# A two-layer diffusion transformer on one core: the build-time clock steps engines when they come free, and loads of gated values keep to three pairs ahead of weights

## The chip, the cores and the metric

The kernel runs on one core of one Trainium2 chip. The core has TensorE (PE, matmuls), VectorE (DVE), ScalarE (ACT), GpSimd (POOL) and SyncE (SP, which here issues DMAs). The metric is the device time of one execution in microseconds; the median of three runs counts.

## The reference

Two transformer layers over 1024 latent tokens and 256 context tokens of width 1024, in fp32. Layer 0 attends in a neighbourhood, layer 1 with grouped queries. Each is followed by a SwiGLU feed-forward of 2816 hidden features; the context runs through the one of layer 0 alone.

```python
def swiglu_ffn(h, w_in, w_out):
    a, g = jnp.split(h @ w_in, 2, axis=-1)
    return (jax.nn.silu(a) * g) @ w_out
...
    for i in range(DEPTH):
        ...
        a_l = ada_norm(h, norm_mix[i], sh1_l, sc1_l)
        ...
        h = h + g1_l * y_l
        h = h + g2_l * swiglu_ffn(ada_norm(h, norm_ffn[i], sh2_l, sc2_l), ffn_w_in[i], ffn_w_out[i])
        if ctx_out:
            hc = hc + g1_c * y_c
            hc = hc + g2_c * swiglu_ffn(ada_norm(hc, norm_ffn[i], sh2_c, sc2_c), ffn_w_in[i], ffn_w_out[i])
    return rms_norm(h, norm_final)
```

## The kernel before

**Stages.** The span goes through the start and layer 0's attention (to about 767 us), layer 0's feed-forward, called FFN0 here (767 to 1697), layer 1's attention (to 2370) and FFN1 (to the end). The change touches the two feed-forwards and the norms at their borders.

**Arithmetic.** A tile x is split into a high part (a cast on ACT to fp32r: `ah` for activations, `wh` for weights, in lines L1189 and L1431) and a low part x − high (`al`, `wl`: L949 on POOL or L952 on DVE, both in the helper `combine`). A product of two fp32 tiles is three fp32r matmuls: high·high, low·high, high·low (L1455 to L1457 in the first stage of a feed-forward, L1698 to L1700 in the second, L1476 to L1478 and L1351 to L1353 for the context).

**A feed-forward.** Both stages split their matrices in 2x2 blocks and form seven products instead of eight from sums and differences of blocks (`PARTS`). The first stage (`mm1`) goes over 22 hidden blocks and writes gated values through `store` to DRAM, as `FA` and `FT` of eleven pairs of hidden blocks. The second (`mm2`) goes over the seven products in the order P7, P1, P6, P3, P2, P5, P4 (`ORDER2`) and, in each, over the eleven pairs; a pair of a product is 12 matmuls of 128x512. For each pair `load_t` loads a gated value and `load_w` one or two weight tiles (`in_fout`); `weight2` and `value2` make high and low parts of them. P7 takes two weight tiles a pair, P1 one.

**Norms.** `norm` squares the columns (L157), adds squares on DVE or POOL (L144), sums over partitions with a matmul by ones (L190, in `ms_sum`), takes Ln and Exp on ACT (L177, L179) and applies the result (L1170, L1180 in a feed-forward; `apply_norm` with L211 and L131 to L134 for layer 1). b=0 and b=1 are the two halves of 512 latent tokens, ctx the context. Silu of the context's hidden blocks is L1322.

**What sets the order.** Each engine runs its instructions in the order in which the program was written, and the program is written by a planner at build time, `Lanes` (here `bg`). It has a clock `bg.now` in ns, a time at which each engine is taken to come free (`busy`), and a list of small generators (a split, a sum, a load), each of which waits for an engine's letter: T and M for matmuls, L and A for ACT, D for DVE, G for POOL. "GD" is given to whichever of POOL and DVE asks first. `turn` is called once for each matmul product of the feed-forwards and moves the clock by 227 ns; an engine whose `busy` is in the past then writes its next instruction. `both` models that DVE and POOL slow each other when they work side by side. Nothing of the clock exists on the chip; there only the written order counts, with semaphores between engines. DMAs stand in SP's queue, in program order and behind the waits of each.

Of the kernel before, what the change touches and what calls it, by code (L numbers as in the profile page):

```python
# [72 lines left out]
def _build(tc, nc, I, O, top):  # L73
# [110 lines left out]
    def ms_sum(acc, added, count, n, bank, stop=False):  # L184
        while len(added) < count or max(added) > bg.now:
            yield ""
        ms, free = yield from bank()
        yield "M"
        for i in range(2):
            t.matmul(ms[:, :n], lhsT=ones[:], rhs=acc[i], start=i == 0, stop=stop and i == 1)  # L190
        return ms[:, :n], free

    def apply_norm(tag, src, rs, G, sh, ah, al, tmp):
# [3 lines left out]
        def split(kc, x, give):  # L197
            yield "A"
            s.activation(ah[:, kc, :], x, AF.Identity, bias=sh(kc))
            yield "GD"  # L200
            norm_lo(bg.engine == "G", al[:, kc, :], x, sh(kc), ah[:, kc, :].bitcast(F32))
            left.discard(kc)
            if bg.engine == "G":
                bg.cost = 3.7 * x.shape[1]
            yield from bg.sleep(2000 if bg.engine == "G" else 700)
            give()

        for kc in range(KC):
            x, give = yield from tmp.take("nx", rs.shape[1])
            yield "D0"  # L210
            v.scalar_tensor_tensor(x, src(kc), G(kc), rs, ALU.mult, ALU.mult)  # L211
            bg.enter(tag, split(kc, x, give), 800, 1)
# [329 lines left out]
    class Lanes:  # L542
# [60 lines left out]
        def both(self, ns):  # L603

            e, o = ("G", "D") if self.engine == "G" else ("D", "G")
            slow = dict(D=2.17, G=1.19)
            left = max(0.0, self.port[o] - self.now)
# [5 lines left out]
            self.port[e] = self.now + self.cost  # L613
# [21 lines left out]
        def turn(self):  # L635
# [4 lines left out]
            for e in "TMLADG":  # L640
                if self.busy.get(e, 0) <= self.now:
                    self.step(e)
# [374 lines left out]
    class Ffn:  # L1017
# [268 lines left out]
        def ctx_norm(self, tiles, rings):  # L1286
# [5 lines left out]
            at = bg.now + 4000  # L1292
# [76 lines left out]
        def load1(self):  # L1369

            fin = I[f"fin{self.layer}"]
            self.tasks = {}
            for i, (j, names, _) in enumerate(self.todo):
# [241 lines left out]
        def load_t(self):  # L1615

            yield from self.said("feed1")
            for x in ORDER2:
                if x == "P4" and self.layer == 0:
                    self.traw.leave(self.acells1, lambda: self.when.update({"act 1": bg.now}))  # L1620
                for i in range(NP):
                    yield from self.known(("F", i, PARTS[x][1]))
# [5 lines left out]
        def load_w(self):  # L1628

            yield from self.said("load1")  # L1630
            fout = I[f"fout{self.layer}"]
            for x in ORDER2:
                for i in range(NP):
                    for k, half in self.RAW2[x]:
# [3 lines left out]
                        self.when["W", x, i, k, half] = bg.now + 3000  # L1638
            self.when["load w"] = bg.now
# [662 lines left out]
    def load_h():  # L2302
        for kc in range(KC):
            dma(out=ffn0.h[0][kc], in_=H0d[0][:, kc, :])
            ffn0.at[0, kc] = bg.now + 6000
            yield from bg.sleep(1000)
# [320 lines left out]
```

## Time and profile before

| | us |
|---|---|
| median of three runs | 3082.59 (3079.08 to 3083.17) |
| profiled execution, own time | 3080.29 |
| its span | 3078.5 |
| PE busy | 2936.6 (95%) |
| DVE busy | 2339.7 (76%) |
| POOL busy | 1807.9 (59%) |
| ACT busy | 1618.8 (53%) |

The own time is that of the whole execution, the span that from its first to its last instruction. Shares are of the span and are averages over stages with different limits: where PE is busy throughout, work on the other engines is hidden; the time over PE's work is in short stretches in which PE stands still, and these are read one by one from the timeline of PE.

### The profile page before, as it was taken

To read this page: it belongs to the slowest core of one execution; us is meant where nothing else is said; L and a number is where in the kernel's file an instruction comes from. 1 tells how busy PE (TensorE), PEld (TensorE's weight loads), DVE (VectorE), ACT (ScalarE), POOL (GpSimd) and SP (SyncE) were. 2 spreads that over 40 slices of the span, in tenths; PEclk is the share of its full clock that TensorE was granted. 3 is DMA by queue.
4 is the path that set the end of the run, shared out by engine and by line. 5 is a ranking of instruction groups with operands and counts; after the bars stand their busy time and mean duration, and the time that the engine had idled before them with its cause. 6 is when DMAs were issued, how large, how long until landed. Compare 5 with 4: busy or idle time off the path is not lost.

```text
span 3078.5 us, 50271 instructions
## 1 busy us (share of the span) xinstructions
PE 2936.6 (95%) x16460; PEld 2511.9 (82%) x16460; DVE 2339.7 (76%) x4291; ACT 1618.8 (53%) x3736; POOL 1807.9 (59%) x1485
## 2 busy tenths in 40 slices
PE   7999999899999999998998899999999989999998
PEld 4888997788788888887878788888888778888786
DVE  7588778775888776567878588899897787666796
ACT  4345555775642222234455488898886622333444
POOL 4246556775685454356776256666644686555775
PEclk8999999999999999999999999999999999999999
DMA  7777777886434554258655523333323333224963
GB/s 262 218 232 236 226 220 225 241 230 210 171 122 159 192 179 168 74 185 298 201 177 188 171 81 96 98 104 105 106 76 121 130 127 127 103 103 152 321 198 113
DMA packets 307173, 519.05 MB, mean 169 GB/s; under 512 B 46433, under 2 KB 112097, under 8 KB 305121
## 3 DMA queue, kind: packets, MB, share of 16 engines
q1 hardware_dynamic: 306912, 515.84, 51.8%
q8 instruction: 131, 2.15, 0.3%
q14 instruction: 130, 1.06, 0.1%
HBM read 389.61 MB, written 120.18 MB: 166 GB/s over the span
## 4 chain that ended last, share of the span: by engine, by line
PE 75%; DVE 10%; DMA 5%; ACT 3%; POOL 3%; issue 2%; SPq 1%; DVEq 0%; POOLq 0%; ACTq 0%
PE pf L1457 9%; PE pf L1455 9%; PE pf L1456 9%; PE T L864 5%; PE o L495 5%; PE pf L1699 4%; PE pf L1700 4%; PE pf L1698 4%; PE ps L767 3%; PE ps L768 3%; PE ps L769 3%; PE S L2235 2%; DMA K<-Kd 2%; PE S L2236 2%; DVE c L952 1%
## 5 line engine op out<-in xcount | busy, mean ns | idle before, releaser
L857 POOL TENSOR_SCALAR Pt<-Pt,rc 128x1280 f32<-128x1280 f32 (+3 forms) x288 | 299.1, 1039 | 389.8 <-ACT pT L872 139.4
L872 ACT CAST pT<-T 128x256 fp32r<-128x256 f32 (+2 forms) x672 | 304.7, 477 | 125.4 <-PE T L864 121.2
L877 DVE TENSOR_TENSOR pT<-T,pT 128x256 fp32r<-128x256 f32 (+2 forms) x672 | 341.7, 534 | 32.9 <-ACT pT L872 32.4
L864 PE MATMUL T<-ident,Pt 128*128 128x128 f32 x1952 | 304.1, 275 | 22.8 <-POOL Pt L857 22.2
L864 PEld LDWEIGHTS T<-ident,Pt 128*128 128x128 f32 x1952 | 236.6, 141 | 78.7 <-POOL Pt L857 34.0
L495 PE MATMUL o<-pT,Vt 128*128 128x256 f32 x1952 | 296.1, 290 | 2.3 <-DVE pT L877 2.2
L767 PE MATMUL ps<-ah,wh 128*128 128x512 f32 (+1 forms) x688 | 261.2, 380 | 5.4 <-ACT ah L430 2.5
L495 PEld LDWEIGHTS o<-pT,Vt 128*128 128x128 f32 x1952 | 254.8, 189 | 9.3 <-DVE pT L877 5.5
L768 PE MATMUL ps<-al,wh 128*128 128x512 f32 (+1 forms) x688 | 251.7, 366 | 3.9 <-POOL al L132 2.2
L769 PE MATMUL ps<-ah,wl 128*128 128x512 f32 (+1 forms) x688 | 251.0, 365 | 2.8 <-DVE wl L336 2.8
L846 ACT ACTIVATE Pt<-S,rc 128x512 f32<-128x512 f32 (+2 forms) x384 | 247.1, 654 | 9.1 <-DVE rc L838 5.8
L949 POOL TENSOR_TENSOR c<-c,c 128x512 fp32r<-128x512 f32 (+1 forms) x120 | 176.0, 1474 | 91.7 <-ACT c L1431 60.0
L2227 DVE TENSOR_REDUCE nm<-S 128x1 f32<-128x512 f32 x256 | 169.6, 682 | 36.4 <-PE S L2236 34.7
L892 POOL TENSOR_TENSOR r<-ob 128x256 f32<-128x256 f32 x144 | 123.8, 859 | 63.1 <-ACT ob L886 57.3
L952 DVE TENSOR_TENSOR c<-c,c 128x512 fp32r<-128x512 f32 (+1 forms) x111 | 128.2, 1168 | 42.3 <-ACT c L1431 24.7
L846 ACT ACTIVATE Pt<-X,rc 128x256 f32<-128x256 f32 x256 | 125.1, 489 | 65.2 <-DVE rc L838 58.5
L949 POOL TENSOR_TENSOR wl<-c,wh 128x512 fp32r<-128x512 f32 x59 | 81.6, 1385 | 120.3 <-ACT wh L1431 113.5
L1431 ACT CAST wh<-c 128x512 fp32r<-128x512 f32 x111 | 68.6, 619 | 157.4 <-POOL c L949 63.9
L769 PEld LDWEIGHTS ps<-ah,wl 128*128 128x128 f32 x688 | 131.2, 191 | 24.4 <-DVE wl L336 3.3
L767 PEld LDWEIGHTS ps<-ah,wh 128*128 128x128 f32 x688 | 131.6, 191 | 18.7 <-ACT ah L430 2.7
L768 PEld LDWEIGHTS ps<-al,wh 128*128 128x128 f32 x688 | 131.7, 191 | 17.3 <-POOL al L132 4.2
L1455 PE MATMUL pf<-c,wh 128*128 128x512 f32 x372 | 144.9, 390 | 0.0
(613 smaller groups left out, 9734.9 us busy)
## 6 DMA issues: line engine op xcount, KB each, us to landing
c<-in_fout SPq DMA_DIRECT2D x119, 256.0 KB, 3.5
wr<-in_wqkv SPq DMA_DIRECT2D x53, 512.0 KB, 4.3
wr<-in_adaT SPq DMA_DIRECT2D x96, 256.0 KB, 3.1
c<-in_fin SPq DMA_DIRECT2D x68, 256.0 KB, 2.9
adaw<-in_adaT SPq DMA_DIRECT2D x64, 256.0 KB, 3.9
wr<-in_wo SPq DMA_DIRECT2D x32, 512.0 KB, 4.2
wr<-in_fin SPq DMA_DIRECT2D x58, 256.0 KB, 2.9
K<-Kd SPq DMA_DIRECT2D x64, 224.0 KB, 4.5
```

The costliest lines, as they stand in the source:

```text
L495: t.matmul(o_ap, lhsT=u.V[:, kb, :], rhs=u.pT[:, i, :], start=i == 0, stop=i == len(u.blocks) - 1)
L767: t.matmul(ps, lhsT=hi[:, c], rhs=ah[:, kc, :n], start=kc == 0, stop=False)
L768: t.matmul(ps, lhsT=hi[:, c], rhs=al[:, kc, :n], start=False, stop=False)
L769: t.matmul(ps, lhsT=lo[:, c], rhs=ah[:, kc, :n], start=False, stop=kc == KC - 1)
L846: s.activation(u.Pt[:, off:off + u.wid[c]], u.S[c], AF.Exp, bias=u.min, scale=u.sign, accum_out=u.rc[:, 3 + c:4 + c])
L857: g.tensor_scalar(Pt, Pt, u.rc[:, 2:3], 1.0, ALU.mult, ALU.mult)
L864: t.transpose(T[:, i * P:(i + 1) * P], u.Pt[:, (i0 + i) * P:(i0 + i + 1) * P], ident[:])
L872: s.copy(u.pT[:, i0:i0 + n, :P], u.T[c])
L877: v.tensor_tensor(u.pT[:, i0:i0 + n, P:], u.T[c], u.pT[:, i0:i0 + n, :P].bitcast(F32), ALU.subtract)
L1455: t.matmul(ps[:], lhsT=r32(hi[:, c]), rhs=bh, start=k == 0, stop=False)
L1456: t.matmul(ps[:], lhsT=r32(hi[:, c]), rhs=bl, start=False, stop=False)
L1457: t.matmul(ps[:], lhsT=r32(lo[:, c]), rhs=bh, start=False, stop=k == 3)
```

## The change

It has four parts.

- `turn` steps an engine if its `busy` lies at most 226 ns ahead of the clock, not only when it lies behind.
- `both` takes other factors for DVE and POOL side by side (2.25 and 1.3), and starts at the time when the engine comes free. `apply_norm` now counts its operations in it, and `ms_sum` writes the sum's matmuls 1200 ns later than the last add.
- `load_t` loads the value of a pair only once the weights of the pair three before it have been asked for (`seen`).
- Three times of the start are moved: the context's norm (+6000 and the word "h2" said), `load1` of layer 0 (waits for "h2"), and `load_h`.

```diff
--- before.py
+++ after.py
@@ -182,7 +182,7 @@
         give()
 
     def ms_sum(acc, added, count, n, bank, stop=False):
-        while len(added) < count or max(added) > bg.now:
+        while len(added) < count or max(added) + 1200 > bg.now:
             yield ""
         ms, free = yield from bank()
         yield "M"
@@ -200,8 +200,9 @@
             yield "GD"
             norm_lo(bg.engine == "G", al[:, kc, :], x, sh(kc), ah[:, kc, :].bitcast(F32))
             left.discard(kc)
+            bg.both((1290 if bg.engine == "G" else 690) * x.shape[1] / 512)
             if bg.engine == "G":
-                bg.cost = 3.7 * x.shape[1]
+                bg.cost += 1.37 * x.shape[1]
             yield from bg.sleep(2000 if bg.engine == "G" else 700)
             give()
 
@@ -209,6 +210,7 @@
             x, give = yield from tmp.take("nx", rs.shape[1])
             yield "D0"
             v.scalar_tensor_tensor(x, src(kc), G(kc), rs, ALU.mult, ALU.mult)
+            bg.both(690 * x.shape[1] / 512)
             bg.enter(tag, split(kc, x, give), 800, 1)
         while left:
             yield ""
@@ -603,14 +605,15 @@
         def both(self, ns):
 
             e, o = ("G", "D") if self.engine == "G" else ("D", "G")
-            slow = dict(D=2.17, G=1.19)
-            left = max(0.0, self.port[o] - self.now)
+            slow = dict(D=2.25, G=1.3)
+            now = max(self.now, self.busy[e])
+            left = max(0.0, self.port[o] - now)
             beside = min(left, ns * slow[e])
             more = min(left * (slow[o] - 1), beside * (1 - 1 / slow[o])) if left else 0.0
             self.busy[o] += more
             self.port[o] += more
             self.cost = ns + beside * (1 - 1 / slow[e])
-            self.port[e] = self.now + self.cost
+            self.port[e] = now + self.cost
 
         def at(self, after, fn):
             heapq.heappush(self.events, (self.now + after, next(self.seq), fn))
@@ -638,7 +641,7 @@
             while self.events and self.events[0][0] <= self.now:
                 heapq.heappop(self.events)[2]()
             for e in "TMLADG":
-                if self.busy.get(e, 0) <= self.now:
+                if self.busy.get(e, 0) <= self.now + 226:
                     self.step(e)
             self.pump(1 / 3)
 
@@ -1289,7 +1292,8 @@
             yield from self.said("h")
             for kc in range(KC):
                 dma(out=self.c2(kc), in_=H0d[2][:, kc, :])
-            at = bg.now + 4000
+            at = bg.now + 6000
+            self.when["h2"] = bg.now
             tmp = Temps(**tiles)
             tmp.rings = rings
             G, sh = self.norm2
@@ -1370,6 +1374,8 @@
 
             fin = I[f"fin{self.layer}"]
             self.tasks = {}
+            if self.layer == 0:
+                yield from self.said("h2")
             for i, (j, names, _) in enumerate(self.todo):
                 q = []
                 for u in "a" if names == ["P1", "P2"] else "ag":
@@ -1615,10 +1621,14 @@
         def load_t(self):
 
             yield from self.said("feed1")
+            while not hasattr(self, "seen"):
+                yield ""
             for x in ORDER2:
                 if x == "P4" and self.layer == 0:
                     self.traw.leave(self.acells1, lambda: self.when.update({"act 1": bg.now}))
                 for i in range(NP):
+                    while self.seen + 3 < ORDER2.index(x) * NP + i:
+                        yield ""
                     yield from self.known(("F", i, PARTS[x][1]))
                     cell = yield from self.traw.take()
                     dma(out=cell, in_=self.Fd[i][PARTS[x][1]])
@@ -1628,7 +1638,7 @@
         def load_w(self):
 
             yield from self.said("load1")
-            fout = I[f"fout{self.layer}"]
+            fout, self.seen = I[f"fout{self.layer}"], 0
             for x in ORDER2:
                 for i in range(NP):
                     for k, half in self.RAW2[x]:
@@ -1636,6 +1646,7 @@
                         dma(out=cell, in_=fout[2 * i + k][:, half * 512:half * 512 + 512])
                         self.wq[x, i, k, half] = cell
                         self.when["W", x, i, k, half] = bg.now + 3000
+                    self.seen += 1
             self.when["load w"] = bg.now
 
         RAW2 = dict(P7=((0, 0), (0, 1)), P6=((1, 1),), P4=((1, 1),), P1=((0, 0),), P2=((1, 0),), P5=((0, 1), (1, 1)), P3=((1, 0),))
@@ -2302,8 +2313,8 @@
     def load_h():
         for kc in range(KC):
             dma(out=ffn0.h[0][kc], in_=H0d[0][:, kc, :])
-            ffn0.at[0, kc] = bg.now + 6000
-            yield from bg.sleep(1000)
+            ffn0.at[0, kc] = bg.now + 7000
+            yield from bg.sleep(1300)
         ffn0.when["h"] = bg.now
 
     def columns(G, sh, w):
```

On each engine the number of arithmetic operations stays, but some 94 additions and subtractions move from POOL (L949) to DVE (L952; 955 in the changed file); ACT has three more table loads. Three places follow at which the prediction looks.

SP's queue at the change from P7 to P1 in the second stage of FFN0. `FT_` and `FA_` are gated values, `in_fout` weights, `H0d` the residual; `rope` and the `c_` are cells that weights are loaded into. Before:

```order
...
L81 DMA al_15217<-FT_10_1224 128x512
L81 DMA al_15217<-FA_0_1152 128x512
L81 DMA al_15217<-FA_1_1159 128x512
...
L81 DMA al_15179<-FA_9_1215 128x512
L81 DMA ah_15178<-FA_10_1222 128x512
L81 DMA ah_15178<-FT_0_1155 128x512
...
L81 DMA ah_15178<-FT_6_1197 128x512
L81 DMA rope<-in_fout 128x512
L81 DMA c_10550<-in_fout 128x512
...
```

Now:

```order
L81 DMA al_15214<-FT_10_1224 128x512
L81 DMA al_15214<-FA_0_1152 128x512
L81 DMA al_15179<-FA_3_1173 128x512
L81 DMA al_15179<-FA_4_1180 128x512
L81 DMA al_15179<-FA_5_1187 128x512
L81 DMA FT_10_1226<-sq 128x512
L81 DMA c_15451<-H0d_122 128x512
L81 DMA c_15464<-H0d_122 128x512
L81 DMA c_10547<-in_fout 128x512
```

Before, 18 loads of gated values stand between the first load of FT_10 and the first weight of P1 (`rope`); now four stand there, with one store and two loads of the residual, ahead of the first weight of P1 (`c_10547`).

ACT's queue in the first stage of FFN0, at the norm's Ln (L177) and Exp (L179) of the latent half b=1 and the Silu of the context (L1322; L1326 in the changed file). Before:

```order
L1431 CAST wh<-wr 128x512
L177 ACTIVATE c_10548<-pf_10553,eps 128x512
L179 ACTIVATE c_10548<-c_10548 128x512
L1322 ACT_TABLE_LOAD
L1322 ACTIVATE c_10503<-pf_10555 128x256
L1431 CAST wh<-wr 128x512
L1431 CAST wh<-rope 128x512
```

Now:

```order
L1313 ACTIVATE ah_11008<-pl,modB_84 128x256
L1326 ACT_TABLE_LOAD
L1326 ACTIVATE c_10503<-pf_10554 128x256
L177 ACT_TABLE_LOAD
L177 ACTIVATE c_10548<-pf_10553,eps 128x512
L179 ACT_TABLE_LOAD
L179 ACTIVATE c_10548<-c_10548 128x512
L1437 CAST wh<-wr 128x512
L1437 CAST wh<-rope 128x512
L1183 ACTIVATE c_10516<-c_10516,modB_84 128x512
```

The Silu with its table load has moved ahead of the Ln, and Ln and Exp each have a table load of their own.

DVE and POOL at the first S3 products in the first stage of FFN1 (`c_26858<-r` is a sum of weight blocks, `wl` the low part of such a sum, the three-letter names of 275 and 276 applied norm blocks). DVE before, and POOL before:

```order
L952 TENSOR_TENSOR c_26857<-c_26837,c_26853 128x512
L952 TENSOR_TENSOR c_27577<-c_26858,c_27576 128x512
L952 TENSOR_TENSOR c_27589<-c_26859,c_27588 128x512
L952 TENSOR_TENSOR c_27602<-c_26861,c_27601 128x512
L952 TENSOR_TENSOR c_26860<-r_26827,r_26828 128x512
L952 TENSOR_TENSOR ah_27608<-r_26828,ah_27608 128x512
L952 TENSOR_TENSOR wl<-c_26858,wh 128x512
```

```order
L949 TENSOR_TENSOR c_26848<-c_26840,c_26844 128x512
L949 TENSOR_TENSOR c_26849<-c_26841,c_26845 128x512
L949 TENSOR_TENSOR c_27596<-c_26860,c_27595 128x512
L949 TENSOR_TENSOR c_26858<-r_26829,r_26827 128x512
L949 TENSOR_TENSOR c_26859<-r_26828,c_26858 128x512
L949 TENSOR_TENSOR wl<-c_26860,wh 128x512
L949 TENSOR_TENSOR c_26861<-r_26830,c_26859 128x512
```

DVE now, and POOL now:

```order
L955 TENSOR_TENSOR c_27553<-c_26859,c_27552 128x512
L955 TENSOR_TENSOR c_27565<-c_26860,c_27564 128x512
L955 TENSOR_TENSOR c_26858<-r_26829,r_26827 128x512
L955 TENSOR_TENSOR ah_27600<-r_26828,ah_27600 128x512
L955 TENSOR_TENSOR c_26872<-c_26871,pf_26876 128x512
L955 TENSOR_TENSOR c_26859<-r_26828,c_26858 128x512
```

```order
L952 TENSOR_TENSOR c_26856<-c_26836,c_26852 128x512
L952 TENSOR_TENSOR c_26849<-c_26841,c_26845 128x512
L952 TENSOR_TENSOR c_27544<-c_26858,c_27543 128x512
L952 TENSOR_TENSOR c_27579<-c_26861,c_27578 128x512
L952 TENSOR_TENSOR c_26860<-r_26827,r_26828 128x512
L952 TENSOR_TENSOR wl<-c_26858,wh 128x512
L952 TENSOR_TENSOR wl<-c_26860,wh 128x512
L952 TENSOR_TENSOR wl<-c_26859,wh 128x512
L952 TENSOR_TENSOR c_26859<-wr 128x512
```

Before, POOL makes the sum c_26858 and DVE its low part `wl`, two operations later; now DVE makes the sum and POOL takes `wl` up soon after it.

## Rows read from the trace of the kernel before

**Rows 1.** Windows: busy us per engine (x instructions), granted clock, DMA share, GB/s.

```profile
825.00:872.00 47.00, 47.00 (x306) 42.82 (x306) 42.72 (x37) 29.70 (x55) 42.26 (x27) 1.00 0.32 104
...
1371.00:1401.00 30.00, 30.00 (x134) 24.83 (x133) 20.08 (x16) 9.53 (x16) 20.11 (x13) 1.00 0.96 340
1401.00:1414.00 13.00, 4.76 (x13) 3.16 (x12) 4.97 (x4) 5.09 (x10) 5.18 (x4) 0.74 1.05 389
1596.00:1678.00 82.00, 69.73 (x524) 64.25 (x524) 76.08 (x67) 48.50 (x86) 69.12 (x44) 1.00 0.65 209
...
2600.00:2700.00 100.00, 100.00 (x443) 82.84 (x442) 63.01 (x79) 32.16 (x54) 48.88 (x37) 1.00 0.29 103
```

**Rows 2.** Timeline of PE, FFN0, second stage: P7 gives way to P1.

```profile
1401.01 0.39 PE L1700 MATMUL pf<-wh,al 128*128 128x512 f32 x1
...
1409.05 0.80 PE L1698 MATMUL pf<-wh 128*128 128x512 f32 x1 [7.65 <-ACT wh L1189]
...
1414.42 0.40 PE L1698 MATMUL pf<-c,c 128*128 128x512 f32 x1
```

**Rows 3.** Timeline of SP (DMA queue) in the same place.

```profile
1390.35 0.32 SPq L81 DMA_DIRECT2D al<-FT  x1
1390.72 5.01 SPq L81 DMA_DIRECT2D al<-FA  x10
...
1396.96 5.09 SPq L81 DMA_DIRECT2D ah<-FT  x7
1402.40 0.33 SPq L81 DMA_DIRECT2D rope<-in_fout  x1
```

**Rows 4.** Chain that ended last, same place.

```profile
1402.40 5.36 DMA rope<-in_fout
```

**Rows 5.** Timeline of SP, FFN1, before P1 of the second stage.

```profile
2860.25 6.48 SPq L81 DMA_DIRECT2D al<-FA  x10
...
2871.19 0.96 SPq L81 DMA_DIRECT2D wr<-in_fout  x2
```

**Rows 6.** Timeline of PE, FFN1, P1 of the second stage.

```profile
2877.84 0.51 PE L1698 MATMUL pf<-al 128*128 128x512 f32 x1 [1.97 <-ACT al L1189]
...
2879.24 0.51 PE L1699 MATMUL pf<-al 128*128 128x512 f32 x1 [0.90 <-POOL al L949]
```

**Rows 7.** Timeline of PE, FFN1, first S3 products.

```profile
2468.98 0.79 PE L1455 MATMUL pf<-ah,wh 128*128 128x512 f32 x1 [9.16 <-ACT wh L1431]
...
2472.23 0.79 PE L1457 MATMUL pf<-ah,wl 128*128 128x512 f32 x1 [2.03 <-DVE wl L952]
```

**Rows 8.** Timelines of POOL and DVE in that stretch.

```profile
2466.57 1.70 POOL L949 TENSOR_TENSOR c<-r,r 128x512 f32<-128x512 f32 x1
...
2444.46 0.68 DVE L952 TENSOR_TENSOR o<-o,pf 128x512 f32<-128x512 f32 x1
...
2447.89 1.77 DVE L952 TENSOR_TENSOR al<-c,ah 128x512 fp32r<-128x512 f32 x1
```

**Rows 9.** Waits of PE, 1596 to 1678 us: total, times, longest.

```profile
PE pf L1353 <- DVE c L952: 6.6, 7, 1.7
```

**Rows 10.** Timeline of PE, FFN0's start: sums of the norm; first S3.

```profile
812.40 3.59 PE L190 MATMUL pf<-c,ones 128*128 128x512 f32 x4 [2.23 <-DVE c L144]
...
876.52 0.50 PE L1455 MATMUL pf<-ah,wh 128*128 128x512 f32 x1 [3.41 <-ACT wh L1431]
```

**Rows 11.** Timeline of ACT, FFN0 (Ln L177, table load and Silu L1322).

```profile
821.86 0.69 ACT L177 ACTIVATE c<-pf,eps 128x512 f32<-128x512 f32 x1
822.57 0.63 ACT L179 ACTIVATE c<-c 128x512 f32<-128x512 f32 x1
823.22 1.28 ACT L1322 ACT_TABLE_LOAD   x1
825.14 0.38 ACT L1322 ACTIVATE c<-pf 128x256 f32<-128x256 f32 x1 [0.64 <-PE pf L1478]
```

**Rows 12.** Chain that ended last, the last 20 us.

```profile
3061.88 1.58 DVE o L144
```

## The prediction

> **What bounds the kernel now.** The page gives PE 95% of the span, so I looked only for stretches in which PE stands still. The timeline of PE gives the pace without stalls: 443 matmuls of 128x512 in 100 us [rows 1], or 0.226 us each, so a pair of twelve takes 2.71 us. Whatever PE takes beyond that in the two feed-forwards is a stall. I went through them in order of time and followed each with the waits of PE and then the timelines of the engine named. The second view matters more than the first, since an engine named is often itself behind another or behind a transfer. Seven places are left.
>
> *The change from P7 to P1 in FFN0.* The last matmul of P7 starts at 1401.01, the first of P1 at 1409.05, the next pair at 1414.42 [rows 2]. Without a stall that pair would start at 1401.24 + 2.71 = 1403.95; lost: 10.5 us. The granted clock of that stretch is 0.74 [rows 1]: PE stood still before and then ran its first matmuls at the lower level (0.80 us for one against 0.39 [rows 2]). PE names ACT, but ACT waits for a weight: its load is issued at 1402.40, lands 5.36 us later [rows 4], and the first matmul follows at 1409.05, 6.65 us after the issue. The queue of SP shows why so late: behind the load at 1390.35 stand ten loads from FA in 5.01 us, one more, and seven from FT in 5.09 us, 18 loads of gated values, and only then the weight [rows 3]. *The same in FFN1* is smaller: weights are issued at 2871.19 behind ten such loads from 2860.25 on [rows 5]; PE waits 1.97 and 0.90 us [rows 6], 2.9 in all, and some 0.5 us more at a lower clock.
>
> *The first S3 products.* In FFN1 PE waits 9.16 us for ACT's high part and 2.03 us for DVE's low part [rows 7]. The high part waits for a sum that POOL makes from 2466.57 on [rows 8]: both vector engines work through a queue of norm and sums. In FFN0 the same place costs 3.41 us [rows 10] and about 1.5 us behind it.
>
> *The norm's sums of FFN0* wait 2.23 us for a late add on DVE [rows 10]. *The end of FFN0* (context's second stage and the norms of layer 1): PE is busy 69.7 of 82 us, DVE 76.1, POOL 69.1 [rows 1]; PE waits 6.6 us for DVE alone [rows 9]. The vector engines bound it. *The tail* is a chain of single operations; the add of 1.58 us stands on it [rows 12].
>
> **The change, part by part.** *Loads of values at most three pairs ahead.* In FFN0 four value loads, one store and two loads of the residual stand between the load of FT_10 and the first weight of P1, instead of 18. SP takes about 0.5 us for one (ten in 5.01 us [rows 3]), so the weight is issued at about 1390.35 + 8 x 0.5 = 1394.4 instead of 1402.40: 8 us earlier. Ready 6.65 us later, at 1401.0, it meets PE at 1401.24. The stall of 7.65 us goes, and with it most of the matmuls at the lower clock: -9, bounds -6 (the landing lengthens by 3 us, since the transfers around share a DMA system that is 0.96 to 1.05 full here [rows 1]) and -10.5. In FFN1 five value loads instead of 17 stand there in the queue; at 0.65 us each (ten in 6.48 us [rows 5]) the weights' issue moves up by 12 x 0.65 = 7.8 us against 2.9 us of waits and 0.5 at the lower clock: -3.5, bounds -1 and -4. The moved transfers are the same bytes; what is late next would be values, but they now have three pairs, 8.1 us, of lead over the weights behind them, against a landing of some 5.4.
>
> *Engines stepped up to 226 ns early, and other factors in the model of the shared port.* On the chip this is a new order. Some 94 operations go from POOL to DVE, half in each feed-forward. Alone, such an operation takes DVE 0.68 us; beside POOL, 1.77 [rows 8]. So 47 of them add 32 us to DVE in a feed-forward of 700 to 900 us, less what it gains where POOL is now idle: each POOL operation beside DVE cost it up to 1.09 us. At PE's full pace DVE is busy 63 of 100 us [rows 1], so it doesn't become the bound of the long stretches. It counts at the vector-bound places:
> - Norm's sums in FFN0: six operations more on DVE, three fewer on POOL: 6 x 0.68 - 3 x 1.09 = +0.8; I take +1, bounds 0 and +4.
> - First S3 of FFN1: POOL has 25 instead of 27 operations in front of the sums (2 x 1.70 = 3.4 less), DVE 41 instead of 40, and the low part follows directly on POOL: -3, bounds 0 and -6.
> - End of FFN0: the sums of norm b=1 come twelve matmuls earlier (12 x 0.226 = 2.7), those of b=0 42 short ones earlier. From there DVE has two operations more (+1.4), POOL three fewer (-5.1 on POOL, up to -3.3 on DVE). I take -3 for the earlier start and -3 for the rest: -6, bounds 0 (raw weights or residuals bound it) and -12 (all idle time of PE, 82 - 69.7).
> - Tail: the last sums come twelve matmuls earlier, so that POOL's scalings are through before DVE's last adds, which then take 0.7 rather than 1.58: -1.5 with two of them, bounds 0 and -2.
>
> *Ln behind Silu in FFN0.* This speaks against the change. Now the Ln starts at 821.86, the Exp ends at 822.57 + 0.63 = 823.20, and the Silu with its load of 1.28 us comes after, waiting for PE until 825.14 [rows 11]. With Silu first: Silu 825.14 to 825.52, load to 826.80, Ln (0.69) to 827.49, load to 828.77, Exp (0.63) to 829.40. The norm's factor is 6.2 us later. Behind it, 47 us of matmuls cover up to the first S3, but DVE and POOL are busy 42.7 and 42.3 us of these [rows 1], so not all of the delay is taken up: +3, bounds 0 and +6.
>
> By the Trainium skill ("ScalarE: Activation LUTs", section "What ACT_TABLE_LOAD costs") a switch costs 1.28 us of load and 1.38 of drain, 2.66 in all; the trace shows the 1.28, and the load starting 0.02 us behind the Exp, without a drain in front. By that page the factor would be 2 x 1.38 = 2.8 us later still, and the term about +4.5.
>
> *Later sums (1200 ns), later context norm and start.* Their effect lies in the same orders and is counted there; the loads of the start reach PE while attention still runs.
>
> Sum: +1 +3 -9 -6 -3 -3.5 -1.5 = -19. The profiled execution takes 3080.29 us, 2.3 less than the median of the runs; 3080.3 - 19 = 3061.3, and as a median 3063.6.
>
> **Rivals.** *(a) Transfers only change places.* DMA is full at 1371 to 1414 [rows 1], so a weight that is issued earlier lands later, and a value is late in its place. Both transfer terms go: -19 + 12.5 = -6.5, 3076. For it: DMA share about 1. Against it: the 18 loads of values in front are not needed by P1's first pairs, so the same DMA carries the urgent one first. *(b) The vector-bound places gain to their bounds:* end of FFN0 -12, first S3 of FFN1 -6, first S3 of FFN0 and sums 0, transfers -14: about -34, 3048.6. *(c) The two late starts cost their bounds and the norms gain nothing:* +4 +6 -12.5 = -2.5, 3080. For it: at the end of FFN0 PE also waits for others than DVE. *(d) Slower: three pairs are too short a window.* If a value's way from issue to use (landing 5.4 us, up to 6.5, a cast of 0.6, a low part of 1.77) is longer than what three pairs give (8.1 us) plus the weights' own lead, every pair is paced by it: about 9 us for three pairs is 3.0 instead of 2.71, 0.29 x 154 pairs = +45, less 19: +26, 3108. It decides where the lead of weights falls below 1 us; at its shortest it is now 6.65 us (P1's first pair, which itself came late), so I give it little.
>
> **How the numbers follow.** Forecast 0.60, (a) 0.10, (b) 0.17, (c) 0.07, (d) 0.06. A measurement of this kernel tells about 0.2%, 6 us, from no change: faster is below 3076.4. Half of (a) is faster, so faster 0.82, same 0.12, slower 0.06. The likeliest is 3063.5, its own range 3056 to 3071. The range over the cases, 3046 to 3078, takes in (b) and (a) and leaves (d) and part of (c) out.
>
> **What would show it.** Right: at the change from P7 to P1, weights issued at once and PE at full pace in both feed-forwards; at the end of FFN0 less idle time of PE; the norm's Exp in FFN0 some 6 us later than the sums would allow. Wrong: a new wait of PE for a value's high part in the second stages (then (d) or (a)); a longer wait at FFN0's first S3 than 5 us more; DVE busy throughout a stretch in which PE waits for a low part.

## The result and the profile after

The changed kernel takes 3059.62 us in the median of four runs (3056.94 to 3063.29), before 3081.99; the ratio is 0.993, with a 95% interval of 0.9912 to 0.9947. It became faster by 22 us where 19 were forecast. The page of its profiled execution (own time 3060.65 us) gives the span and each engine's busy time:

```profile
span 3058.9 us, 50273 instructions
...
PE 2925.4 (96%) x16460; PEld 2507.1 (82%) x16460; DVE 2350.2 (77%) x4385; ACT 1618.0 (53%) x3739; POOL 1677.4 (55%) x1391
```

PE's busy time fell by 11 us and the span by 20, POOL's busy time by 130, DVE's grew by 10.

But for the norms' sums over partitions, PE runs the same 16420 matmuls in the same order in both kernels. So the time between the starts of two matmuls, the same two in each kernel, gives the time of a stage. The table is worked out in this way from PE's timelines, in us; each stage ends with the start of a matmul of the named place, the same in each kernel.

```
stage (ends where)                               before   after   change   forecast
attention 0, the same program                     749.6   753.2    +3.6       0
three norms of FFN0 (first context product)        67.0    65.0    -2.0      +1
to FFN0's first S3, 13 matmuls into it             62.6    65.5    +2.9      +3
rest of the first stage, P7                       517.8   517.9    +0.1       0
P7 to P1, FFN0 (ends in P1's fifth pair)           22.3    11.8   -10.5      -9
rest of the second stage                          154.8   156.5    +1.7       0
end of FFN0                                       104.2   101.0    -3.2      -6
attention 1, its output, FFN1's norms             728.2   725.8    -2.4       0
FFN1's first S3                                    69.0    64.8    -4.2      -3
rest of the first stage, P7                       391.0   389.9    -1.1       0
P7 to P1, FFN1 (ends in P1's seventh pair)         26.1    22.7    -3.4      -3.5
rest of the second stage                          143.1   143.1     0         0
tail                                               27.1    26.1    -1.0      -1.5
```

Attention 0 is the same program in all kernels here, and took 747.7 to 758.2 us in their profiled executions; so the total of one execution says nothing of changes below some 10 us. Without attention 0 the change is -23 us. The single stages repeat better: kernels with one order on PE, DVE, POOL and ACT (before and e2; changed and e1; e7, e10 and e11) differ among themselves by at most 0.9 us in the stage to FFN0's first S3, 1.6 at the end of FFN0, 1.5 at FFN1's first S3 and 2.6 at the three norms.

**P7 to P1.** PE's timeline shows the last matmul of P7, the first of P1 and the first of the next pair (line numbers of the changed file):

```profile
1405.55 0.39 PE L1711 MATMUL pf<-wh,al 128*128 128x512 f32 x1
1405.78 0.39 PE L1709 MATMUL pf<-wh 128*128 128x512 f32 x1
...
1408.50 0.39 PE L1709 MATMUL pf<-c,c 128*128 128x512 f32 x1
```

No wait is left where [rows 2] had 7.65 us, and the matmul takes 0.39 us at a granted clock of 1.00 (1404 to 1420 us), the higher of its two levels. SP's queue at the time:

```profile
1389.98 0.38 SPq L81 DMA_DIRECT2D rope<-in_fout  x1
1390.41 0.45 SPq L81 DMA_DIRECT2D c<-in_fout  x1
1391.27 0.33 SPq L81 DMA_DIRECT2D al<-FT  x1
1391.64 1.86 SPq L81 DMA_DIRECT2D al<-FA  x4
...
1396.19 0.95 SPq L81 DMA_DIRECT2D c<-in_fout  x2
```

By the order of the queue, the 22 weight loads of P7 end ahead of 1389.98, so the two loads at 1389.98 and 1390.41 are P1's first two weights. They stand in front of the load of FT_10 and are issued 15.8 us before their use, where [rows 3] had the first at 1402.40 behind 18 value loads. Those at 1396.19, which the prediction (and the order shown ahead of it) took for the first, belong to the third and fourth pair. In FFN1 seven value loads, counted from FT_10 on, stand in front of P1's first weight, where the prediction had five; the same count gives 17 before, as it had. By the same order of the queue, the weights behind the first five values are P7's last two, and P1's first two are these:

```profile
2849.88 1.00 SPq L81 DMA_DIRECT2D al<-FA  x2
2851.26 0.98 SPq L81 DMA_DIRECT2D c<-in_fout  x2
```

They are issued 9.3 us before their use (2860.56). Against the last matmul of P7 that is 4.8 us earlier than before, not 7.8. FFN1 answers to [rows 6], without a wait:

```profile
2860.33 0.39 PE L1711 MATMUL pf<-al,ah 128*128 128x512 f32 x1
2860.56 0.39 PE L1709 MATMUL pf<-wh,al 128*128 128x512 f32 x1
```

**FFN0's start.** ACT's timeline answers to [rows 11]:

```profile
823.73 1.28 ACT L1326 ACT_TABLE_LOAD   x1
826.62 0.38 ACT L1326 ACTIVATE c<-pf 128x256 f32<-128x256 f32 x1 [1.61 <-PE pf L1484]
827.01 1.28 ACT L177 ACT_TABLE_LOAD   x1
828.30 0.69 ACT L177 ACTIVATE c<-pf,eps 128x512 f32<-128x512 f32 x1
829.01 1.28 ACT L179 ACT_TABLE_LOAD   x1
830.31 0.63 ACT L179 ACTIVATE c<-c 128x512 f32<-128x512 f32 x1
```

The Ln begins at 828.30, 1.5 us after the prediction's 826.80, as the Silu does (826.62 against 825.14), and the Exp ends at 830.94. The norm's sums end at 818.13, so the Exp is 12.8 us behind them instead of 7.2: 5.6 us later, where 6.2 were forecast. Each load took 1.28 us; Ln and Exp began 0.01 and 0.02 us behind theirs: no drain beside the load shows here either, so that the trace goes by 1.28 for a switch, not by the 2.66 of the Trainium skill ("ScalarE: Activation LUTs", section "What ACT_TABLE_LOAD costs"). PE's waits behind it (825 to 900 us: total, times, longest):

```profile
PE pf L1463 <- DVE wl L955: 6.4, 3, 4.5
PE pf L1463 <- POOL wl L952: 1.3, 1, 1.3
```

These are waits for low parts, 7.7 us in four of them, where [rows 10] had one of 3.41 us for a high part at the S3 itself. DVE shows where the delay went. It stands still until a cast that waits behind the Exp in ACT's order has ended, makes the low part of that cast, and then begins to apply the norm:

```profile
831.48 0.69 DVE L955 TENSOR_TENSOR wl<-wr,wh 128x512 fp32r<-128x512 f32 x1 [5.60 <-ACT wh L1437]
```

The waits of PE at the three norms before it (744 to 825 us) moved rather than went; the longest is now at the context's sums:

```profile
PE pf L190 <- DVE c L144: 8.0, 2, 5.4
```

**End of FFN0, FFN1's first S3, tail.** At the end of FFN0 (1585 to 1670 us) PE waits for DVE 4.7 us instead of 6.6 [rows 9], for the norm's sums 0.3:

```profile
PE pf L1357 <- DVE c L955: 4.7, 6, 1.8
PE pf L1357 <- POOL c L952: 3.1, 2, 1.7
PE pf L190 <- DVE y L144: 0.3, 1, 0.3
```

At FFN1's first S3, 9.16 and 2.03 us [rows 7] became:

```profile
PE pf L1461 <- ACT wh L1437: 7.2, 1, 7.2
PE pf L1463 <- POOL wl L952: 0.9, 1, 0.9
```

In the tail, two adds of DVE take 1.48 us together, where [rows 12] has 1.58 for one:

```profile
3042.33 1.48 DVE L144 TENSOR_TENSOR o<-o,o 128x512 f32<-128x512 f32 x2
```

### The profile page after: what moved, and what is told of

Read it like the earlier page. It is cut to its first block, busy times and chain, and to the rows that moved or that the text cites. A ratio compares the mean times of both kernels' runs of the same rounds, so it can differ in the third digit from the quotient of the medians.

```text
span 3058.9 us, 50273 instructions
## 1 busy us (share of the span) xinstructions
PE 2925.4 (96%) x16460; PEld 2507.1 (82%) x16460; DVE 2350.2 (77%) x4385; ACT 1618.0 (53%) x3739; POOL 1677.4 (55%) x1391
## 5 line engine op out<-in xcount | busy, mean ns | idle before, releaser
L952 POOL TENSOR_TENSOR c<-c,c 128x512 f32<-128x512 f32 (+1 forms) x105 | 157.2, 1504 | 109.6 <-DVE c L955 42.4
L955 DVE TENSOR_TENSOR c<-c,c 128x512 fp32r<-128x512 f32 (+1 forms) x126 | 137.3, 1100 | 52.2 <-ACT c L1437 36.9
L1461 PE MATMUL pf<-c,wh 128*128 128x512 f32 x376 | 146.5, 390 | 0.0
L1462 PE MATMUL pf<-c,wh 128*128 128x512 f32 x376 | 146.5, 390 | 0.0
```

The source lines that it names most:

```text
L1461: t.matmul(ps[:], lhsT=r32(hi[:, c]), rhs=bh, start=k == 0, stop=False)
L1462: t.matmul(ps[:], lhsT=r32(hi[:, c]), rhs=bl, start=False, stop=False)
```

## The experiments

Twelve kernels ran. Ratios are to the kernel before in the same run on the same chip, with 95% intervals. The intervals are 5 to 14 us wide, so kernels whose intervals overlap are told apart by their stages and not by their medians. `S3` is the stretch "to FFN0's first S3" of the table above. `Exp` says how long after the norm's sums of b=1 have ended the Exp of its factor ends, from ACT's and PE's timelines.

```
kernel              median us  ratio   95% interval      P7-P1 FFN0, FFN1   end FFN0   Exp     S3
before                  -        -           -               22.3   26.1      104.2    7.2    62.6
changed              3059.6    0.9930  0.9912-0.9947         11.8   22.7      101.0   12.8    65.5
e1_no_window         3072.8    0.9965  0.9953-0.9977         17.4   28.3      100.5   13.7    65.4
e2_window_only       3065.2    0.9947  0.9935-0.9960         11.8   22.7      103.7    7.3    61.7
e3_ln_first          3061.6    0.9931  0.9918-0.9943         11.8   22.7       99.8   10.3    62.4
e4_step_only         3077.5    0.9984  0.9976-0.9993         20.1   28.6      104.5    7.1    59.7
e5_step_old          3067.9    0.9955  0.9938-0.9972         11.8   22.7      105.6   17.1    68.4
e6_port_old          3064.2    0.9941  0.9919-0.9964         11.8   22.7      100.7   13.6    66.4
e7_no_sum_wait       3052.2    0.9906  0.9888-0.9924         11.8   22.7       99.7    6.1    58.8
e8_start_old         3055.4    0.9915  0.9898-0.9932         11.8   22.7      103.6    6.0    58.9
e9_late_factor       3058.8    0.9914  0.9899-0.9929         11.8   22.7      101.3   10.7    64.1
e10_window_0         3054.9    0.9901  0.9885-0.9918         11.8   22.7      101.3    6.0    58.7
e11_window_8         3053.4    0.9900  0.9885-0.9915         11.8   22.7      100.9    6.1    58.7
e12_start_sum_old    3052.8    0.9897  0.9882-0.9912         11.8   22.7       97.0    7.0    60.0
```

### e1_no_window: the change without the limit on loads of values

```diff
                 for i in range(NP):
-                    while self.seen + 3 < ORDER2.index(x) * NP + i:
-                        yield ""
                     yield from self.known(("F", i, PARTS[x][1]))
```

> The changed kernel without the limit of three pairs on loads of gated values; the orders of PE, ACT, DVE and POOL are those of the changed kernel, only SP's queue has 18 value loads in front of P1's first weight again. Theory (the limit alone brings weights early): both stalls at the change from P7 to P1 come back, +9.8 in FFN0 and +4.8 in FFN1 by the traces, so about 3074 us, and PE waits 7 us for a weight's high part there. Rival (the stepped clock made the room, the limit adds nothing): within 3 us of the changed kernel, 3060 to 3063.

3072.8 us, and 5.6 us more at each of the two places: the limit is what takes the stalls away. But in FFN0 only half comes back. SP's queue shows P1's first two weights at 1391.99 and 1392.42, in front of the 18 values, with those of the third pair only behind, at 1409.46:

```profile
1391.99 0.38 SPq L81 DMA_DIRECT2D rope<-in_fout  x1
1392.42 0.47 SPq L81 DMA_DIRECT2D c<-in_fout  x1
...
1393.62 6.16 SPq L81 DMA_DIRECT2D al<-FA  x10
...
1400.86 5.16 SPq L81 DMA_DIRECT2D ah<-FT  x7
...
1409.46 0.94 SPq L81 DMA_DIRECT2D c<-in_fout  x2
```

PE accordingly does P1's first two pairs without a wait and then stands still at the third:

```profile
1415.88 0.51 PE L1707 MATMUL pf<-c,c 128*128 128x512 f32 x1 [2.50 <-ACT c L1192]
1417.29 0.50 PE L1708 MATMUL pf<-c,c 128*128 128x512 f32 x1 [0.90 <-POOL c L952]
```

The first matmul of the third pair starts 6.4 us after its weight was asked for, as P1's first did before (6.65 us). So in the changed kernel only about half of the 10.5 us in FFN0 hangs on the limit: without it, the other parts of the change already put two weights ahead of the values. The limit alone gives the whole 10.5 (e2), so the two overlap. The stepped clock alone doesn't move the two weights ahead (e4); which other part does was not tried. In FFN1 it is the other way round: there the stretch without the limit, 28.3 us, is 2.2 longer than in the kernel before.

### e2_window_only: the kernel before with the limit alone

The lines of `seen` in `load_t` and `load_w` of the change, nothing else.

> The kernel before with the limit of three pairs alone. Theory: PE meets P1's first weights without a stall in both feed-forwards, -9.8 and -4.8, so about 3067.5 us, and nothing else moves. Rival (transfers only change places, DMA is full there): values are late in place of weights, 3078 to 3083.

3065.2 us, a little better than the theory. The stages that were to move did, by -10.5 and -3.4, to the very times of the changed kernel; the others stayed within 2.4 us of before, attention 0 aside. P1's first weights are issued at 1394.00 behind three values, where the prediction's step had 1394.4:

```profile
1394.00 0.38 SPq L81 DMA_DIRECT2D rope<-in_fout  x1
```

They are used 8.2 us later, at 1402.15, without a wait. That transfers only change places is refuted: no wait of PE for a value shows in the second stages. (The one wait there, 0.6 us at 2849.88, is for a weight's low part, and the kernel before has it too.)

### e3_ln_first: the first Silu held back until the factor is there

```diff
             sa = self.run[j, "sa"] = yield from self.sa.take()
+            yield from self.said(("rs", 1))
             yield "A"
             s.activation(sa, ps[:, :256], AF.Silu)
```

(`apply` sets "rs" when it is given the factor.)

> The changed kernel with the first Silu of the context held back until the norm of b=1 has its factor, so that Ln and Exp come first and the three extra table loads are gone. Theory (the late factor costs +2.9 net: 8.4 us of new waits for low parts at 839 to 876, 5.5 of which come back at the first S3): about 3056.7 us, with waits in front of the first S3 as in the kernel before. Rival (the delay is covered, the waits come from the new order of DVE and POOL): 3059 to 3061, the waits for low parts stay.

The median doesn't show the gain (3061.6, ratio 0.9931 against 0.9930), nor could it tell 3 us. The stretch took 62.4 us instead of 65.5, the expected 3. PE's waits there (825 to 900 us) for low parts fell from 7.7 us to 1.8, and a wait for a high part came back, as in the kernel before:

```profile
PE pf L1463 <- ACT wh L1439: 2.3, 1, 2.3
PE pf L1465 <- DVE wl L955: 1.8, 2, 1.2
```

The experiment was less clean than meant, since a cast took the Silu's place in front of the Ln and came late itself; the profile doesn't say what held it up:

```profile
832.54 0.62 ACT L1439 CAST wh<-wr 128x512 fp32r<-128x512 f32 x1 [2.82 <-issue]
833.06 0.68 ACT L177 ACTIVATE c<-pf,eps 128x512 f32<-128x512 f32 x1
833.78 0.63 ACT L179 ACTIVATE c<-c 128x512 f32<-128x512 f32 x1
```

Without any table load in front, the Ln is still 8.9 us behind the sums (which end at 824.13).

### e4_step_only: the kernel before with the stepped clock alone

```diff
-                if self.busy.get(e, 0) <= self.now:
+                if self.busy.get(e, 0) <= self.now + 226:
                     self.step(e)
```

> The kernel before with engines stepped up to 226 ns early and nothing else. Theory (the new order gives what is left beside the limit, at the end of FFN0, at FFN1's start and in the tail, 3 to 9 us): 3073 to 3079 us, with the stalls at P7 to P1 as before and no extra table loads. Rival 1 (those gains need the new factors of the shared port): 3080 to 3084. Rival 2 (the step gives the gains of the transfers as well): below 3070.

3077.5 us, as the theory had it. FFN1's first S3 (65.7 us), the tail (26.1) and FFN0's first S3 (59.7) gain, the end of FFN0 does not. The stall at P7 to P1 stays (1380 to 1440 us), and it is at the first pair:

```profile
PE pf L1698 <- ACT c L1189: 5.1, 1, 5.1
PE pf L1699 <- POOL c L949: 0.6, 1, 0.6
```

### e5_step_old, e6_port_old: the change without the step, and without the new model of the port

```diff
# e5_step_old
-                if self.busy.get(e, 0) <= self.now + 226:
+                if self.busy.get(e, 0) <= self.now:
# e6_port_old
-            slow = dict(D=2.25, G=1.3)
-            now = max(self.now, self.busy[e])
-            left = max(0.0, self.port[o] - now)
+            slow = dict(D=2.17, G=1.19)
+            left = max(0.0, self.port[o] - self.now)
```

> The changed kernel with engines stepped only when they are free (the step of the kernel before), all else as changed. Theory (the stepped clock gives the 4 us at FFN1's first S3 and 1 us in the tail, the port's factors and the later sums give the 3 us at the end of FFN0): about 3064 us, FFN1's first S3 as in the kernel before, the end of FFN0 as in the changed one. Rival (the step gives all of these): about 3068, all three as before.

> The changed kernel with the old factors and the old start time in the model of the shared port (the norm's operations still counted in it). Theory (these make the 3 us at the end of FFN0): the stretch from the last products to layer 1's first takes 104 us rather than 101, total about 3063 us. Rival (the norm's counted operations or the later sums make it): 101 us there, total 3059 to 3061.

Both theories fell on the end of FFN0: 105.6 us without the step, 100.7 with the old port. Taken out of the change, the step costs the gain there, but alone it doesn't bring it (e4: 104.5). Without the step the factor of b=1 is 17.1 us behind the sums, and the first S3 costs 68.4; FFN1's first S3 takes 67.0 us, between the changed kernel's 64.8 and the 69.0 of before, and the tail 25.9, so that the tail's gain stays without the step. With the old port model FFN1's first S3 takes 66.7 us, 1.9 more than in the changed kernel, and the rest of FFN1's second stage 144.8, as in e4; in all other kernels that stage takes 142.8 to 143.2. So the step with the old port model costs 1.7 us there, and the new model takes it away. The differences at the other stages are no larger than those between executions of one order.

### e7_no_sum_wait, e8_start_old, e12_start_sum_old: the change without its other times

```diff
# e7_no_sum_wait (and e12)
-        while len(added) < count or max(added) + 1200 > bg.now:
+        while len(added) < count or max(added) > bg.now:
# e8_start_old (and e12)
-            at = bg.now + 6000
+            at = bg.now + 4000
-            if self.layer == 0:
-                yield from self.said("h2")
-            ffn0.at[0, kc] = bg.now + 7000
-            yield from bg.sleep(1300)
+            ffn0.at[0, kc] = bg.now + 6000
+            yield from bg.sleep(1000)
```

> The changed kernel with the norm's sums written right after the last add, without the 1200 ns. Its ACT order has Ln before the first Silu of the context again, and no extra table loads. Theory (the sums then stand in PE's queue before their adds are done on the chip): longer waits of PE for the adds at the norms, +1 to +3 at FFN0's three norms and the two of FFN1, -3 at FFN0's first S3 for the earlier factor; together 3057 to 3061 us. Rival (the place of the sums doesn't matter, only the factor's): -3, about 3056.5.

> The changed kernel with the old times of FFN0's start (the residual's loads, the context's norm, the weights not held back). Ln stands before the first Silu again. Theory: at the sums of b=0 PE waits 5 us for the adds as in the kernel before, the 6 us of wait at the context's sums go, and the first S3 gains 3 us: FFN0's start 3 us shorter in all, about 3056.5 us. Rival (the three norms together stay, and the factor isn't earlier in fact): 3059 to 3061.

> The kernel of e7_no_sum_wait with the old times of FFN0's start as well: limit, step and port factors of the change stay. Theory (the start's times only move waits from the sums of b=0 to those of the context; with the factor early either way): the three norms together within 1 us of e7_no_sum_wait's 64.0, the first S3 59, total 3051 to 3056. Rival (the old times spare a wait, since the context's sums no longer wait 6 us): 3047 to 3050, the fastest of all.

Each of them puts Ln in front of Silu again, and each has a lower median than the changed kernel: 3052.2, 3055.4 and 3052.8 us. The intervals of e7 and e8 overlap with that of the changed kernel, e12's touches it; but the stretch to the first S3, 58.8 to 60.0 us instead of 65.5, is shorter beyond the spread of that stage. With e7 the stretch to the first S3 takes 58.8 us, 6.7 less than in the changed kernel, twice what either side of its expectation had, and the sums of the norms didn't suffer: the three norms of FFN0 take 64.0 us instead of 65.0. ACT and PE's waits (825 to 900 us) of e7:

```profile
821.39 0.68 ACT L177 ACTIVATE c<-pf,eps 128x512 f32<-128x512 f32 x1
822.10 0.63 ACT L179 ACTIVATE c<-c 128x512 f32<-128x512 f32 x1
822.75 1.28 ACT L1326 ACT_TABLE_LOAD   x1
```

```profile
PE pf L1463 <- POOL wl L952: 2.4, 1, 2.4
```

The old times of the start only move the wait between the sums of b=0 and of the context: 64.9 us for the three norms in e8, 65.3 in e12. So the start's new times bring nothing at the norms. And since either e7 or e8 alone puts Ln first, it is the 1200 ns and the new start times together that put Silu first in the changed kernel. e8's gain of 6.6 us at the first S3 is in part given back at the end of FFN0 (103.6 us against 101.0); e12 has the shortest time there, 97.0, and what brings it was not tried.

### e9_late_factor: the delay by itself

```diff
# on e7
         yield "L"
+        if tag == ("norm", 0, 1):
+            s.activation(rs, ms, AF.Silu)
         s.activation(rs, ms, AF.Ln, bias=eps[:])
```

> The kernel of e7_no_sum_wait with one Silu more on ACT right before the Ln of the norm b=1 of FFN0, on the same tile that the Ln then overwrites; nothing else moves on any engine. It brings three table loads (1.28 us each) and 0.7 us of work, so the factor comes 4.5 us later. Theory (from here on each us of the factor's delay is a us of time, as the kernels so far line up): the stretch to the first S3 takes 63.3 us rather than 58.8, total about 3056.7. Rival (47 us of matmuls cover it): 58.8 to 60, total 3052.

The orders of PE, DVE, POOL and SP are those of e7. ACT does what was meant, in 5.8 us instead of 1.3:

```profile
818.22 1.28 ACT L178 ACT_TABLE_LOAD   x1
819.51 0.60 ACT L178 ACTIVATE c<-pf 128x512 f32<-128x512 f32 x1
820.13 1.28 ACT L179 ACT_TABLE_LOAD   x1
821.42 0.69 ACT L179 ACTIVATE c<-pf,eps 128x512 f32<-128x512 f32 x1
822.13 1.28 ACT L181 ACT_TABLE_LOAD   x1
823.42 0.63 ACT L181 ACTIVATE c<-c 128x512 f32<-128x512 f32 x1
```

DVE waits for the factor:

```profile
824.09 2.08 DVE L1175 SCALAR_TENSOR_TENSOR c<-c,G,c 128x512 f32<-128x512 f32 x3 [3.00 <-ACT c L181]
```

The Exp ends 10.7 us behind the sums instead of 6.1, and the stretch takes 64.1 us instead of 58.8: 5.3 us for 4.6. (The ratios, 0.9914 and 0.9906, don't tell the two apart; the stretch does.) PE's waits there, the first of them e7's:

```profile
PE pf L1465 <- POOL wl L954: 2.4, 1, 2.4
PE pf L1465 <- DVE wl L957: 1.6, 1, 1.6
PE pf L1463 <- ACT wh L1439: 0.8, 1, 0.8
```

### e10_window_0, e11_window_8: the size of the limit

```diff
# on e7; e10, e11
-                    while self.seen + 3 < ORDER2.index(x) * NP + i:
+                    while self.seen < ORDER2.index(x) * NP + i:
+                    while self.seen + 8 < ORDER2.index(x) * NP + i:
```

> The kernel of e7_no_sum_wait with a value loaded only when the weights of the pair before it have been asked for (no pairs ahead instead of three). Theory (weights are asked for 14 to 35 us ahead, so a value has more than its 8 us even so): second stages as with three pairs, total 3050 to 3055. Rival (three pairs are near the point where values pace the products): PE waits for values' high parts in P1 to P4, some 0.3 us or more for each of 154 pairs, 3090 or more.

> The kernel of e7_no_sum_wait with eight pairs instead of three. Eleven values then stand in front of P1's first weight in FFN0, where there are four with three pairs and 18 without a limit. Theory (what counts is the weight's place in the queue): at 0.5 us for each, P7 to P1 takes 3 to 4 us more than the 11.8 of three pairs, but less than the 17.4 without a limit; FFN1 1 to 5 us more; total 3056 to 3060. Rival (the limit counts only as it spreads the DMA, place does not matter): as three pairs, 3052.

None, three and eight pairs do the same: 11.8 and 22.7 us, without any wait of PE in the second stages. For eight pairs my theory fell: the weights of the third pair stand behind eleven values and are issued at 1391.80, but they are used 9.0 us after that (P1 begins at 1395.33, its third pair 5.44 later), more than the 6.65 us that a weight needed before. With three pairs it is 15 us (e7: 1387.01, used at 1402.21). So 9.0 us from issue to use cost nothing, and 6.4 us cost a wait of 2.5 (e1); no kernel lies between.

## Why the prediction was right, point by point

**P7 to P1, both feed-forwards: right, with a wrong detail.** -9 and -3.5 were forecast, -10.5 and -3.4 measured, and e1 and e2 show the limit as the cause. The step "the weight is issued at about 1394.4" holds for the limit alone (1394.00 in e2). In the changed kernel it failed: it took the loads behind the values for P1's first weights, which in fact stand in front of them; nothing is as tight as "ready at 1401.0, it meets PE at 1401.24" had it, and e11 shows some 2 us of slack even with eight pairs. FFN1's term has the same kind of error (five values for seven, 7.8 us for 4.8) and came out even so, since PE's stall there was only 2.9 us and some lower clock. Of the second stage's rest, 1.7 us more come with the stepped order (154.8 us in e2, 156.5 to 156.8 in the kernels with the step), which the sum did not have.

**FFN0's first S3: +3 forecast, +2.9 measured, by two errors that cancel.** "Not all of the delay is taken up: +3" took half of the 6.2 us for covered. In the table above, the kernels with the step line up to about 1 us: the Exp 6.1, 10.3, 12.8, 13.6, 13.7 us behind the sums, the stretch 58.8, 62.4, 65.5, 66.4, 65.4. e9, in which nothing else moves, gives 5.3 us of time for 4.6 of delay. So none of it is covered. The prediction read its spare time from the kernel before (DVE busy 42.72 of 47 us, [rows 1]); a window of e7 between the factor and the first S3 (busy us of PE, PEld, DVE, ACT and POOL) has 0.4 us of 46 to spare on DVE:

```profile
830.00:876.00 46.00, 43.48 (x281) 39.33 (x280) 45.57 (x37) 26.78 (x51) 42.72 (x26) 1.00 0.30 100
```

In all, the late factor costs 6 to 7 us (changed kernel against e7). The other side is a gain that the prediction did not have: the stepped order is 2 to 3 us shorter here (62.6 and 61.7 without it, before and in e2; 59.7 with it in e4, at the same lateness of the Exp). That the sum of the two met the forecast is luck. One of the prediction's signs of being wrong came near: between 831.48 and the end of PE's wait of 4.5 us for DVE's low part (862.5) DVE stands still only once for longer than 0.4 us, 2.42 us behind POOL.

**The 1200 ns: not "counted there".** The prediction put the later sums aside as contained in the orders. Taking them out (e7) moves the Ln ahead of the Silu and wins 7 us. Taking the start's new times out (e8) does the same, so the loss belongs to the two together.

**Norms of FFN0: +1 forecast, -2.0 measured.** Only the wait at b=1 was looked at; the larger waits at b=0 (4.7 us, gone) and at the context's sums (5.4 us, new) were not in the sum, and nearly cancel.

**End of FFN0: -6 forecast, -3.2 measured,** within its bounds and over-sized. Which part brings it is open: with the step it took 97.0 to 104.5 us (103.6 in e8), without 103.7 to 105.6, and e7, e10 and e11 with one order on the engines 99.7 to 101.3.

**FFN1's first S3 and tail:** -3 and -1.5 forecast, -4.2 and -1.0 measured; the step alone gives -3.3 and -1.0 (e4), the rest of the change without it -2.0 and -1.2 (e5), so the two overlap. The executions of one order differ by 1.3 us at the S3 and 1.7 in the tail (before and e2), so the sizes are rough. The price of 0.68 us for an operation of DVE alone, which several terms of the sum use, is read from a row that isn't alone: beside 2444.46 in [rows 8] POOL runs from 2444.11 on, and the DVE operation has a `pf` operand. The figure holds even so (0.69 us at 2441.96, with POOL idle).

**The rivals.** *(a)* is refuted by e2, *(d)* by e10: even without a pair of lead no value is late. *(b)* fell on the end of FFN0, -3.2 us where it had -12, and on FFN1's first S3, -4.2 for -6; its time is nearly reached by e7 and e12 (3052.2 and 3052.8 us), but by the earlier factor. *(c)* was right in that the late factor costs its bound of 6 us and somewhat more, and wrong on the rest: the norm's sums cost no 4 us and the norms gained.

**The total.** 19 us were forecast and 22 measured. The mechanism of the largest terms was right. That the whole came so near is in part luck: the end of FFN0 fell short by 2.8 us and the second stage of FFN0 by 1.7, and the norms (3.0), FFN1's first S3 (1.2) and P7 to P1 of FFN0 (1.5) gave more than forecast. Layer 1's attention took 2.4 us less; it took 725.8 to 730.1 in all these kernels, and no cause for its differences was sought.

## What to carry to other kernels

When several streams share one in-order DMA queue, look at what stands in front of the most urgent load, not at the share of the DMA: here the DMA was full before ([rows 1]) and after (share 0.97 from 1361 to 1391 us, 1.04 from 1391 to 1404), and taking loads that were not yet needed (18 of them in FFN0) out of the way of the urgent ones was worth 14 us (e2). Count the delay of a value on which everything hangs (a norm's factor) in full if the engines behind it are busy without a gap; cover by PE's work was no cover here, where the vector engines had to catch up. And try each of the times in a change by itself: a margin of 1200 ns, together with new times of the start, cost 7 of the 29 us that the change brings without the margin.

## What the runs showed of the hardware that was not expected

An Ln and an Exp behind a Silu took a table load each (827.01 and 829.01 in the changed kernel), 1.28 us every time, though before the change both ran without a load [rows 11]: there ACT's last table load before them is a preload at 2.89 us. And the same program of attention 0 took 747.7 to 758.2 us in fourteen profiled executions, more than most of the terms that were to be told apart; the time between the same two matmuls repeats far better where PE doesn't wait (11.8 us for P7 to P1 in eleven of the kernels) and to 1 or 2 us where it does, and e3, whose median said nothing, could be read from such times alone.
